# Where the matmuls' two operands start in a partition: weights at multiples of 512 bytes, the four input tiles at four other places

## Chip, core and metric

The kernel runs on one core of a Trainium2 chip. What counts is the device time in microseconds (us) of one execution. Matmuls run on TensorE (PE in the profile, its loads of the stationary operand PEld), the rest on VectorE (DVE), ScalarE (ACT) and GpSimd (POOL); SP only issues transfers. "Start" below always means the byte in a partition of the on-chip memory at which a tile begins, taken modulo 512.

## What is computed

Two decoder layers on 256 positions of width 2048, in float32. Each layer is a norm, one wide input projection, attention heads, a gate and an output projection that is added to the residual; a last norm follows. Cut to what matters here:

```
def layer_even(x, norm_g, w_in, w_out):
    h = rmsnorm(x, norm_g)
    qa, ka, va, iq, ik, iw, qb, kb, vb, gate = split_cols(h @ w_in, SPLIT0)
    ...   # two kinds of attention: o_a, o_b
    y = concatenate([o_a, o_b])
    return x + (y * silu(gate)) @ w_out
# layer_odd: the same with two other kinds of attention; then rmsnorm(x, norm_f)
```

## The kernel before

The work is a list of 39 jobs: 14 slices of the first input projection (heads B0 to B5, keys K, index I0 and I1, pairs A0 to A8), four of its output projection (P0 to P3), 17 of the second input projection (C0, F1, G1, C2 to C7, D0 to D7), and four of its output (Q0 to Q3). A job multiplies 256 rows by up to 512 columns over 16 blocks of depth 128 (`kt`). For each `kt` and each half `th` of the rows, `product` (L297 to L299) issues three matmuls that add into one PSUM tile. Every one has its own load of a 128x128 stationary operand, and this text calls the three a triple:

```
    nc.tensor.matmul(o, a, wh, ...)   # L297: stationary xh (or yh), moving whi
    nc.tensor.matmul(o, a, wl, ...)   # L298: stationary xh (or yh), moving wlo
    nc.tensor.matmul(o, b, wh, ...)   # L299: stationary xl (or yl), moving whi
```

Each operand is thus kept as a high and a low part in fp32r. `xh`, `xl` are the normed input of a layer's input projections, `yh`, `yl` the gated heads' output for the output projections. `whi`, `wlo` are the parts of the weights: a piece of weights lands in `raw` (1 MB, issued by SP in `load`), ACT copies it to `whi` (L263) and DVE subtracts to get `wlo` (L264), four buffers of each, up to three halves of a piece ahead of the matmuls. The first job's weights land in `w0yh`, `w0yl`, which lie in the place of `yh`, `yl`. In the last job, Q3, the weights of the first eight `kt` are put into the dead `xh`, `xl`, which are then the moving operand.

Heads run beside the projections as generators: `advance` lets them issue a few small matmuls between triples, in an order written out by `yield` counts. All instructions are in a hand-set order; where tiles lie changes no instruction.

Tiles are laid one behind the other: pool `cp` first, then `wp` (`raw`, `whi`, `wlo`), then `hp` (heads). Each size is rounded up to 32 bytes. The first tile of `cp` starts at 128. Adding up the declared sizes gives the starts before:

| tiles | start mod 512 |
|---|---|
| `cons`, `rt`, `xs` | 128 |
| `xh`, `xl`, `yh`, `yl` (16,384 bytes each, slices of 512 bytes) | 224 |
| `score` (1,536 bytes), `cT` (1,024) | 160, 288 |
| `raw`, `whi`, `wlo` (slices of 2,048 bytes at 512 columns) | 288 |
| `ikh`, `ikl`, `vA`, `tris`, `qkh`, `qkl` of the heads | 288 |
| `ih`, `il`, `sph`, `spl` of the heads | 480 |

A slice of 336 columns (job K) is 1,344 bytes, so that the second `kt` of a buffer starts at 288 + 1,344 = 96 mod 512; one of 264 columns (F1) at 320. `cT` holds a transposed sum of F1's forget gates; DVE writes it once (L657), and POOL sends it to DRAM (L658). `score` holds the index scores and then the mask of the A heads.

Of the kernel before, what the change touches and what calls it, by code (L numbers as in the profile page):

```python
# [7 lines left out]
F32 = mybir.dt.float32  # L8
BF16 = mybir.dt.bfloat16
F32R = mybir.dt.float32r  # L10
# [4 lines left out]
P = 128  # L15
NT = 2
SEQ = 256
D = 2048
KT = D // P
HD = 128  # L20
HA, HB, HC, HDD = 10, 6, 8, 8
# [132 lines left out]
    return np.ascontiguousarray(t.reshape(NT, P, -1).transpose(1, 0, 2).reshape(P, -1))  # L154


@with_exitstack
def trunk(ctx, tc, x, xT, g1, w0, wo0, w1, wo1, bf, gf, consts, rope, out):
    nc = tc.nc
    cp = ctx.enter_context(tc.tile_pool(name="cp", bufs=1))  # L160
# [4 lines left out]
    pa = ctx.enter_context(tc.tile_pool(name="pa", bufs=2, space=PSUM))  # L165
    ctx.enter_context(tc.manual_schedule())

    cons = cp.tile([P, CW], F32, name="cons")
    rt = cp.tile([P, NT, RW // 2], F32, name="rt")
    xs = cp.tile([P, NT, D], F32, name="xs")  # L170
# [10 lines left out]
    nmask = cons[:, 640:1024]  # L181
    bmask = cons[:, 1024:1408]
    smask = cons[:, 1408:1792]
    xh = cp.tile([P, KT, SEQ], F32R, name="xh")
    xl = cp.tile([P, KT, SEQ], F32R, name="xl")
    home = [cp.tile([P, KT * SEQ], F32, name=f"w0{n}", tag=n) for n in ("yh", "yl")]
    ys = []
    ss = cp.tile([P, 3, NT, 5], F32, name="ss")
    rstd = cp.tile([P, 3, NT], F32, name="rstd")
    mhalf = cp.tile([P, NT], F32, name="mhalf")  # L190
# [12 lines left out]
    score = cp.tile([P, 384], F32, name="score")  # L203
    nbA = score
    logf = cp.tile([P, NT, HDD], F32, name="logf")
    cq = cp.tile([P, NT, HDD], F32, name="cq")
    cT = cp.tile([HDD, SEQ], F32, name="cT")
    cTd = dr.tile([HDD, SEQ], F32, name="cTd")
    r0, r1, r2 = rstd[:, 0, :], rstd[:, 1, :], rstd[:, 2, :]
    BLK = ((0, slice(0, P)), (1, slice(P, 384)))  # L210
# [638 lines left out]
```

## Time and profile before

| | |
|---|---|
| time, median of 3 runs | 941.61 us (941.05 to 941.75) |
| time of the profiled execution | 941.87 us |
| its span | 940.1 us |
| PE busy, PEld busy | 925.9 us, 774.2 us |
| DVE, ACT, POOL busy | 591.5, 479.7, 43.9 us |
| matmuls | 4538 |

A matmul's length in the profile is that of one pass from its start to its modelled end, and consecutive ones overlap. What one costs in a stream is the distance between two starts, which the timeline shows to 0.01 us.

### The profile page before, as it was taken

What the parts mean: (1) busy time and instruction counts of PE and PEld (TensorE: products, weight loads), DVE (VectorE), ACT (ScalarE), POOL (GpSimd) and SP (SyncE); (2) the same over time, 40 slices, a digit from 0 to 9 for tenths busy, and PEclk for the clock granted to TensorE, in tenths of its full rate; (3) what the DMA queues carried; (4) which work ended last, traced back from release to release, by engine and by line L of the source; (5) the groups of instructions that cost most, each with busy time, mean ns of one, the idle gap of its engine ahead of it and who ended that gap; (6) DMA issues with size and microseconds to landing.
All of it is one profiled execution on the core that took longest, in us unless ns stands there. A gap on an engine that the chain in (4) does not pass through costs nothing.

```text
span 940.1 us, 11922 instructions
## 1 busy us (share of the span) xinstructions
PE 925.9 (98%) x4538; PEld 774.2 (82%) x4538; DVE 591.5 (63%) x978; ACT 479.7 (51%) x804; POOL 43.9 (5%) x63
## 2 busy tenths in 40 slices
PE   8899999999999999999999999999999999999996
PEld 5888888888888888888898888888888888888886
DVE  7467777766565665555567666666666666665552
ACT  7554454445445545545455555555555544554441
POOL 0002100000000000000000000000000000001110
PEclk9999999999999999999999999999999999999999
DMA  9765344443444445555456444445655555455542
GB/s 345 287 224 180 135 174 169 167 170 136 171 180 179 140 174 180 179 179 180 128 168 245 161 160 158 166 174 179 230 185 185 170 174 172 176 176 179 182 176 90
DMA packets 27177, 168.76 MB, mean 180 GB/s; under 512 B 3160, under 2 KB 3696, under 8 KB 8944
## 3 DMA queue, kind: packets, MB, share of 16 engines
q1 hardware_dynamic: 25920, 165.10, 49.7%
q0 software_dynamic: 768, 2.12, 0.8%
q8 instruction: 35, 0.57, 0.2%
q10 hardware_dynamic: 432, 0.79, 0.2%
q14 instruction: 22, 0.18, 0.1%
HBM read 165.89 MB, written 2.11 MB: 179 GB/s over the span
## 4 chain that ended last, share of the span: by engine, by line
PE 93%; DMA 3%; issue 2%; ACT 1%; DVE 1%; POOL 0%; SPq 0%; POOLq 0%; ACTq 0%; DVEq 0%
PE pj L297 28%; PE pj L299 28%; PE pj L298 28%; PE tp L355 3%; DMA raw<-in_w_in_dram 1%; DMA w0yl<-in_w_in_dram 1%; PE o L382 1%; PE o L383 1%; PE o L381 1%; ACT sq L421 1%; PE s L398 1%; DMA xst<-in_xT_dram 1%; PE s L372 0%; PE s L370 0%; PE s L371 0%
## 5 line engine op out<-in xcount | busy, mean ns | idle before, releaser
L264 DVE TENSOR_TENSOR wlo<-raw,whi 128x1024 fp32r<-128x1024 f32 (+3 forms) x300 | 356.2, 1197 | 223.6 <-ACT whi L263 223.3
L263 ACT ACTIVATE whi<-raw 128x1024 fp32r<-128x1024 f32 (+3 forms) x300 | 304.7, 1025 | 172.6 <-PE pj L299 155.6
L297 PE MATMUL pj<-whi,xh 128*128 128x512 f32 (+3 forms) x992 | 390.9, 394 | 0.9 <-ACT whi L263 0.9
L299 PE MATMUL pj<-whi,xl 128*128 128x512 f32 (+3 forms) x992 | 381.2, 384 | 0.0
L298 PE MATMUL pj<-wlo,xh 128*128 128x512 f32 (+3 forms) x992 | 379.5, 383 | 1.0 <-DVE wlo L264 1.0
L299 PEld LDWEIGHTS pj<-whi,xl 128*128 128x128 f32 x992 | 187.1, 189 | 37.9
L298 PEld LDWEIGHTS pj<-wlo,xh 128*128 128x128 f32 x992 | 187.7, 189 | 33.0 <-DVE wlo L264 1.8
L297 PEld LDWEIGHTS pj<-whi,xh 128*128 128x128 f32 x992 | 187.6, 189 | 32.3 <-ACT whi L263 2.3
L297 PE MATMUL pj<-whi,yh 128*128 128x512 f32 (+1 forms) x248 | 97.1, 392 | 0.0
L299 PE MATMUL pj<-whi,yl 128*128 128x512 f32 (+1 forms) x248 | 95.5, 385 | 0.0
L298 PE MATMUL pj<-wlo,yh 128*128 128x512 f32 (+1 forms) x248 | 94.8, 382 | 0.0
L299 PEld LDWEIGHTS pj<-whi,yl 128*128 128x128 f32 x248 | 46.6, 188 | 10.1
L298 PEld LDWEIGHTS pj<-wlo,yh 128*128 128x128 f32 x248 | 46.7, 188 | 9.0
L297 PEld LDWEIGHTS pj<-whi,yh 128*128 128x128 f32 x248 | 46.7, 188 | 8.2
L407 ACT ACTIVATE pr<-sn,nm 128x128 f32<-128x128 f32 (+1 forms) x48 | 21.5, 448 | 46.2 <-DVE nm L405 46.2
L391 ACT ACTIVATE yh<-tp 128x256 fp32r<-128x256 f32 x32 | 12.3, 384 | 47.1 <-PE tp L355 47.1
L632 DVE RECIPROCAL e<-e 128x256 f32<-128x256 f32 x16 | 28.0, 1753 | 0.5
L350 POOL TENSOR_TENSOR qk<-rot,rot 128x256 f32<-128x256 f32 x22 | 16.0, 741 | 239.2 <-DVE rot L349 239.2
L392 DVE TENSOR_TENSOR yl<-tp,yh 128x256 fp32r<-128x256 f32 x32 | 13.5, 423 | 19.9 <-ACT yh L391 19.9
L421 ACT ACTIVATE sq<-xs 128x512 f32<-128x512 f32 x23 | 14.3, 622 | 22.8 <-DVE xs L589 22.7
L364 ACT ACTIVATE qkh<-tp 128x384 fp32r<-128x384 f32 x22 | 10.8, 491 | 20.5 <-PE tp L355 20.5
L618 ACT ACTIVATE qk<-pj,rr 128x128 f32<-128x128 f32 x32 | 11.8, 368 | 15.9 <-PE pj L299 15.9
(201 smaller groups left out, 704.7 us busy)
## 6 DMA issues: line engine op xcount, KB each, us to landing
raw<-in_w_in_dram SPq DMA_DIRECT2D x108, 1024.0 KB, 4.8
raw<-in_w_out_dram SPq DMA_DIRECT2D x32, 1024.0 KB, 4.8
raw<-in_w_in_dram SPq DMA_DIRECT2D x4, 672.0 KB, 11.9
raw<-in_w_in_dram SPq DMA_DIRECT2D x4, 528.0 KB, 3.5
w0yl<-in_w_in_dram SPq DMA_DIRECT2D x4, 512.0 KB, 7.2
xs<-in_x_dram SPq DMA_DIRECT2D x2, 1024.0 KB, 11.9
raw<-in_w_in_dram SPq DMA_DIRECT2D x4, 512.0 KB, 3.9
xst<-in_xT_dram SPq DMA_DIRECT2D x6, 256.0 KB, 6.6
```

The costliest lines, as they stand in the source:

```text
L263: nc.scalar.activation(hi, rw, AF.Copy)
L264: nc.vector.tensor_tensor(lo, rw, hi.bitcast(F32), op=OP.subtract)
L297: nc.tensor.matmul(o, a, wh, start=(kt == 0), stop=False)
L298: nc.tensor.matmul(o, a, wl, start=False, stop=False)
L299: nc.tensor.matmul(o, b, wh, start=False, stop=(kt == KT - 1))
L350: nc.gpsimd.tensor_tensor(dst, t1[:, 0:n], t2[:, 0:n], op=OP.add)
L355: nc.tensor.transpose(pt[:, i * P:(i + 1) * P], s, ident)
L391: nc.scalar.activation(yh[:, kt, :], pt[:, 0:SEQ], AF.Copy)
L392: nc.vector.tensor_tensor(yl[:, kt, :], pt[:, 0:SEQ], yh[:, kt, :].bitcast(F32), op=OP.subtract)
L407: nc.scalar.activation(pr[:, s], sn[:, s], AF.Exp, scale=-1.0, bias=nm[:, th:th + 1], accum_out=l[:, th:th + 1])
L421: nc.scalar.activation(j, xs[:, th, c * 512:(c + 1) * 512], AF.Square, accum_out=ss[:, i, th, c:c + 1])
L632: nc.vector.reciprocal(e, e)
```

## The change

Four things, all of them about places:

- `xh`, `xl` and the homes of `yh`, `yl` are allocated first in `cp`, with fillers between, so that they start at 128, 256, 384 and 192.
- `cT` is no tile of its own any more but the first eight partitions and 256 columns of `score`.
- A filler of 672 bytes at the end of `cp` lets `wp` and `hp` start at a multiple of 512. Adding up sizes: `yl` ends at 192, the tiles from `cons` to `cq` bring the end to 352, and 672 bytes more make a multiple of 512. So `raw`, `whi`, `wlo` and the first tiles of `hp` start at 0; everything in `wp` and `hp` has moved by 224 bytes. `cons`, `rt`, `xs` start at 192.
- No instruction is added, removed or moved.

```diff
+PHASES = {"xh": 128, "xl": 256, "yh": 384, "yl": 192}
...
+    at, first = 128, {}
+    for n, ph in PHASES.items():
+        if ph != at:
+            cp.tile([P, (ph - at) % 512 // 4], F32, name=f"fill_{n}")
+        first[n] = cp.tile([P, KT * SEQ], F32R if n[0] == "x" else F32, name=n if n[0] == "x" else f"w0{n}", tag=n)
+        at = ph
+    xh, xl = (first[n].rearrange("p (a b) -> p a b", a=KT) for n in ("xh", "xl"))
+    home = [first[n] for n in ("yh", "yl")]
+    ys = []
...
-    xh = cp.tile([P, KT, SEQ], F32R, name="xh")
-    xl = cp.tile([P, KT, SEQ], F32R, name="xl")
-    home = [cp.tile([P, KT * SEQ], F32, name=f"w0{n}", tag=n) for n in ("yh", "yl")]
-    ys = []
...
-    cT = cp.tile([HDD, SEQ], F32, name="cT")
+    cT = score[0:HDD, 0:SEQ]
+    cp.tile([P, 168], F32, name="fill")
```

## Rows read from the trace of the kernel before

**Rows 1.** The page: span, and the share of each engine (busy us, share of the span, instructions).

```profile
span 940.1 us, 11922 instructions
PE 925.9 (98%) x4538; PEld 774.2 (82%) x4538; DVE 591.5 (63%) x978; ACT 479.7 (51%) x804; POOL 43.9 (5%) x63
PEclk9999999999999999999999999999999999999999
```

**Rows 2.** The chain that ended last, by engine; and three transfers of it at the start of the span (start us, length us, what).

```profile
PE 93%; DMA 3%; issue 2%; ACT 1%; DVE 1%; POOL 0%; SPq 0%; POOLq 0%; ACTq 0%; DVEq 0%
...
2.12 4.78 DMA xst<-in_xT_dram
7.28 7.26 DMA w0yl<-in_w_in_dram
17.25 13.83 DMA raw<-in_w_in_dram
```

**Rows 3.** Groups of PE's matmuls by shape: line, out<-moving,stationary, stationary shape, output, count | busy us, mean ns of one | idle before.

```profile
L297 PE MATMUL pj<-whi,xh 128*128 128x512 f32 x896 | 361.6, 404 | 0.9 <-ACT whi L263 0.9
L297 PE MATMUL pj<-whi,yh 128*128 128x512 f32 x232 | 92.7, 399 | 0.0
L297 PE MATMUL pj<-whi,xh 128*128 128x336 f32 x32 | 10.9, 342 | 0.0
```

**Rows 4.** Timeline of PE in the first pass of Q3 (start us, length us, line, what): the first and the last of 19 consecutive matmuls, stationary `yh`, `yl`.

```profile
915.52 0.40 PE L297 MATMUL pj<-whi,yh 128*128 128x512 f32 x1
...
919.64 0.39 PE L297 MATMUL pj<-whi,yh 128*128 128x512 f32 x1
```

**Rows 5.** Timeline of PE in job I1, with a triple of the index heads between two of the projection.

```profile
85.27 0.40 PE L297 MATMUL pj<-whi,xh 128*128 128x512 f32 x1
...
85.95 0.39 PE L528 MATMUL s<-ikh,ih 128*128 128x512 f32 x1
...
86.64 0.39 PE L297 MATMUL pj<-whi,xh 128*128 128x512 f32 x1
...
87.33 0.40 PE L297 MATMUL pj<-whi,xh 128*128 128x512 f32 x1
```

**Rows 6.** Timeline of PE in a C job: two 256-column matmuls of the stick head, and triples behind them.

```profile
586.15 0.28 PE L693 MATMUL s<-sph,tris 128*128 128x256 f32 x1
...
586.39 0.40 PE L297 MATMUL pj<-whi,xh 128*128 128x512 f32 x1
...
587.09 0.40 PE L297 MATMUL pj<-whi,xh 128*128 128x512 f32 x1
...
589.89 0.40 PE L297 MATMUL pj<-whi,xh 128*128 128x512 f32 x1
```

**Rows 7.** Timeline of PE in Q3, 256 columns: seven triples with moving `whi`, then eight with moving `xh`, `xl`, then seven with `whi` again (the starts of first and last).

```profile
923.20 0.28 PE L297 MATMUL pj<-whi,yh 128*128 128x256 f32 x1
...
925.67 0.28 PE L297 MATMUL pj<-whi,yh 128*128 128x256 f32 x1
...
926.03 0.28 PE L297 MATMUL pj<-xh,yh 128*128 128x256 f32 x1
...
928.89 0.28 PE L297 MATMUL pj<-whi,yh 128*128 128x256 f32 x1
...
931.37 0.28 PE L297 MATMUL pj<-whi,yh 128*128 128x256 f32 x1
```

**Rows 8.** Timeline of PE in Q3, 512 columns, moving `xh`: one triple at 908.80 and two at 911.58.

```profile
908.80 0.40 PE L297 MATMUL pj<-xh,yh 128*128 128x512 f32 x1
...
909.50 0.40 PE L297 MATMUL pj<-xh,yh 128*128 128x512 f32 x1
...
911.58 0.39 PE L297 MATMUL pj<-xh,yh 128*128 128x512 f32 x1
...
912.93 0.39 PE L297 MATMUL pj<-xh,yh 128*128 128x512 f32 x1
```

**Rows 9.** Timeline of PE in job K, 336 columns. The buffer's first `kt` starts at 288, its second at 96; each has two triples. Four triples from 29.64, and eight from 35.19.

```profile
29.64 0.32 PE L297 MATMUL pj<-whi,xh 128*128 128x336 f32 x1
...
30.56 0.31 PE L297 MATMUL pj<-whi,xh 128*128 128x336 f32 x1
...
31.48 0.32 PE L297 MATMUL pj<-whi,xh 128*128 128x336 f32 x1
...
35.19 0.32 PE L297 MATMUL pj<-whi,xh 128*128 128x336 f32 x1
...
36.10 0.32 PE L297 MATMUL pj<-whi,xh 128*128 128x336 f32 x1
...
37.04 0.32 PE L297 MATMUL pj<-whi,xh 128*128 128x336 f32 x1
...
37.96 0.32 PE L297 MATMUL pj<-whi,xh 128*128 128x336 f32 x1
...
38.89 0.32 PE L297 MATMUL pj<-whi,xh 128*128 128x336 f32 x1
```

**Rows 10.** Groups of ACT and DVE by shape (as rows 3): the splits of weights with source and target at different starts.

```profile
L263 ACT ACTIVATE whi<-raw 128x1024 fp32r<-128x1024 f32 x276 | 289.2, 1056 | 156.5 <-PE pj L299 146.2 <-ACT whi L263 6.6 <-ACT pT L412 2.0
L263 ACT ACTIVATE xh<-raw 128x1024 fp32r<-128x1024 f32 x4 | 4.0, 1046 | 0.0
L264 DVE TENSOR_TENSOR wlo<-raw,whi 128x1024 fp32r<-128x1024 f32 x276 | 338.8, 1236 | 204.4 <-ACT whi L263 204.2
L264 DVE TENSOR_TENSOR wlo<-w0yl,whi 128x1024 fp32r<-128x1024 f32 x4 | 4.9, 1225 | 0.0
```

**Rows 11.** One stretch (from:to us, length, busy us and instructions of PE, PEld, DVE, ACT, POOL, granted clock, share of the DMA engines, GB/s): in it a piece lands in `raw`.

```profile
587.10:589.80 2.70, 2.70 (x13) 2.22 (x12) 1.08 (x2) 1.56 (x2) 0.00 (x0) 1.00 1.01 416
```

**Rows 12.** All instructions on `score` and on `cT` (duration min/median/max ns, first and last start us): the last reader of `score`, the writer and the reader of `cT`.

```profile
L405 DVE CUSTOM_DVE_ANT_0 sn<-s,score x20: 282/355/421, 210.2 to 318.3; 128x128 f32<-128x128 f32 x10, 128x256 f32<-128x256 f32 x10
...
L657 DVE COPY cT<-s x1: 402/402/402, 493.6 to 493.6; 8x256 f32<-8x256 f32 x1
L658 POOL DMA_DIRECT2D cTd<-cT x1: 558/558/558, 494.3 to 494.3; - x1
```

## The prediction

> **What bounds the kernel now.** I read the page's engine shares first, then the chain that ended last, then the groups of matmuls by shape, then the timeline of PE at single places. The shares say that PE has work in flight for 925.9 of 940.1 us and that its granted clock is at 90% or more of 2.4 GHz in all 40 slices [rows 1]. The chain says the same from behind: 93% of it is PE, 3% transfers [rows 2]. So only two things can move the time by more than a little: the distance between two matmul starts, and the first 30 us, in which transfers are on the path. No other engine's speed matters, since ACT is busy for 51% and DVE for 63% of the span [rows 1].
>
> The groups give the counts: 896 triples of 512 columns with `xh`, `xl` and 232 with `yh`, `yl`, so 1,128; the 32 of 336 columns and the other narrow ones are a few per cent of the work [rows 3]. The group's 404 ns is no price, since passes overlap. The price is in the timeline: six triples in a row take 919.64 - 915.52 = 4.12 us, so a triple takes 686.7 ns and a matmul 228.9 [rows 4]. 512 columns at 2.4 GHz are 213.3 ns, so 15.6 ns of every matmul are something else. All that this change can give or take on PE is in that remainder: 1 ns a matmul is 1,128 x 3 = 3.4 us, 0.36% of the time.
>
> **What the change does to PE.** While one matmul streams its moving operand, PE loads the next one's stationary operand. What the change alters is how far apart the two start. I write d for the start of the stationary minus the start of the moving tile, modulo 512. Before, d is 224 - 288 = 448 for all four inputs. After, the weights start at 0, so d is 128 for `xh`, 256 for `xl`, 384 for `yh`, 192 for `yl`. The trace of before has other values of d in other matmuls, and these are the nearest rows:
>
> - d = 192 (index heads: 480 - 288). Their triple takes 86.64 - 85.95 = 0.69 us, between projection triples at d = 448 of 0.68 and 0.69 [rows 5]. No difference; this is `yl`'s new value.
> - d = 320 (stick heads, 288 - 480, 256 columns): two matmuls take 586.39 - 586.15 = 0.24 us [rows 6]. At d = 448, seven triples of 256 columns take 2.47 us, 117.6 ns a matmul [rows 7], two of them 0.235. No difference.
> - d = 0 (Q3, where `xh`, `xl` move and `yh`, `yl` are stationary, 256 columns): eight triples take 2.86 us, 357.5 ns each, between neighbours of 352.9 and 354.3 [rows 7]. That is 1.1% more, with the same stationary tiles. So starts are not without effect. At 512 columns the same pair gives 0.70 us for one triple and 0.675 for each of two others [rows 8].
> - d = 128 (job K, a buffer's second `kt`, which starts at 96): pairs of triples take 0.94 and 0.93 us against 0.91 and 0.92 for d = 448 in between, 2.2% more; but from 29.64 the two d take 0.92 and 0.92 [rows 9]. Until 31.08 ACT and DVE still wait for the transfer that starts at 17.25 [rows 2], so the difference later may be theirs. This is `xh`'s new value.
>
> d = 256 and 384 are in no row. Three values are equal to each other within what the rows resolve (448, 192, 320), one is worse by 1% on the whole but better in two triples (0), one is unclear (128). The remainder of 15.6 ns itself is there at d = 448, 192 and 320 alike, so it is not a matter of d. I take 0 for the 1,128 wide triples; the bounds are the fastest and the slowest triple seen, 675 and 700 ns, or -12 and +13 ns a triple.
>
> The slow triple occurs at d = 448 too: behind the stick head's matmuls four triples take 589.89 - 587.09 = 2.80 us, 700 ns each [rows 6]. What sets it off there is what came before, since the starts are the same as ever.
>
> The Trainium skill (TensorE: Matmul & The Clock Gate, step-by-step of what each phase is for) says that PE has two independent read ports, one for the moving operand and one for the load, and that loading the next operand takes no bandwidth from the running matmul. By that alone the change is worth 0 and the 1.1% of `xh` in Q3 could not be; the trace shows it, so the measurement decides, and I keep the bounds.
>
> **The other parts.** Splits: ACT takes 1056 ns with source and target at 288 and 1046 with the target at 224; DVE takes 1236 and 1225 with other sources [rows 10]. At most 1%, on engines that PE's work covers; without that cover, 10 ns for each of 276 + 276 would be 5.5 us, but ACT and DVE idle before these splits for 156 and 204 us. 0.
>
> Transfers: pieces land in `raw` at 0 instead of 288. Three transfers of 4.78 + 7.26 + 13.83 = 25.9 us are on the path at the start [rows 2]. With `raw` at 288 a stretch shows the DMA engines fully busy at 416 GB/s [rows 11], so a start that is no multiple of 512 does not hold them far below their best. I take -0.2 us, with 0 and -0.8 (3% of 25.9) as bounds.
>
> `cT` in `score`: the last reader of `score` is DVE at 318.3 us; DVE itself writes `cT` at 493.6, and POOL's transfer reads it at 494.3 [rows 12]. No later instruction writes `score`. DVE does both in its order, so no wait is added on any queue. 0.
>
> Narrow and mixed places: in K the second `kt` now starts at 320 and d becomes 128 - 320 = 320, one of the quiet values which returns 20 ns in some of its 8 pairs of triples, 0.1 us; in Q3 d becomes 256, 128 or 64 instead of 0, 16 triples at 4.6 ns, 0.1 us. Taken as -0.1 together, bounds -0.2 and +0.2.
>
> **The sum.** 941.87 (the profiled execution: 940.1 of span and 1.8 around it) + 0 - 0.2 - 0 - 0.1 = 941.6; the median of the runs lies 0.26 lower than that execution, so 941.3 against 941.61. I forecast no change that can be told: about 0.2% (1.9 us) is what a measurement of this kernel can tell. This case's own range is 939.7 to 943.5.
>
> **Rivals.**
>
> *Faster, because collisions go.* If the load and the stream hinder each other where they come near, then d = 448 is only 64 bytes from d = 0, and all new values are further away. For it: d = 0 does cost 1.1% [rows 7], and the 700 ns triples would be a collision that a small shift in time brings about. Removing only what is seen to collide (some 60 triples of 13 ns, the edges around the heads) gives 1 to 2 us; if the wide triples also go from 686.7 to the 675 of two triples [rows 8], 1,128 x 11.7 ns = 13.2 us, 928. I put it halfway at 934. Against it: 448, 192 and 320 give the same triple, so distance does nothing beyond 64 bytes.
>
> *Faster, because a start at a multiple of 512 is read faster.* 256 more columns cost 228.9 - 117.6 = 111.3 ns [rows 4, 7], 0.435 a column, where 2.4 GHz gives 0.417. If the 4.3% above it came from starts inside a 512-byte row, 0.018 x 512 = 9.3 ns would go from each of 3,384 matmuls: 31 us, 910. Against it: moving starts of 288 and 480 have the same price [rows 5, 6], and a price by column is not what a first row cut short would give. The Trainium skill (TensorE: Matmul & The Clock Gate, back-to-back issue gap) gives N / 2.4 + 2.5 ns, 215.8 for 512 columns; by it the stream has 13 ns too much, and an estimate with it for all 3,384 would be 44 us less. No run here shows a 512-column stream at that distance.
>
> *Slower, because the new distances collide.* The place is `xh`: d = 128 is the value that looked slow in K [rows 9], and it holds for L297 and L299's streams. If two of three matmuls in 896 triples go to the price of the 700 ns triple, that is 2/3 x 13.3 x 896 = 7.9 us, 949.3; with all four inputs colliding 1,128 x 13.3 = 15 us, 956. It decides as soon as the mean triple is over 688.4 ns (1.9 us / 1,128 = 1.7). Against it: the first part of K shows nothing of it, and three of the four values with clean rows are quiet.
>
> **Chances.** No change that can be told 0.40; collisions go 0.26; fast rows 0.08; new collisions 0.26. So faster 0.34, same 0.40, slower 0.26. The predicted time is 941.3. The range takes in half a price beyond the collision rivals on both sides but neither extreme (910; 956): 927 to 951, which leaves out about 0.08 below and 0.07 above, with a little on each side for prices that no row shows.
>
> **What would show it.** Right: the triple in Q3's first pass at 686 to 688 ns, the groups of PE with the same means, the first matmul of job K at the same time within 0.5 us. The rivals show in the same place: 675 or 700 ns a triple in projections with `xh`, and then a difference between `xh` jobs (d = 128, 256) and `yh` jobs (384, 192) tells which d it is; a distance near 219 ns in all of them would be the rows. The forecast is wrong if the triples lock differently over long stretches: what sets off the 700 ns behind the stick heads is not understood, and it could appear or vanish behind any head with the new starts.

## The result and the profile after

The changed kernel takes 951.66 us (median; 951.44 to 952.32), the kernel before beside it 941.68 (941.05 to 942.27). The ratio is 1.0107, its 95% interval 1.0091 to 1.0123: slower by 1.07%, 9.98 us. The forecast was no change, 941.3, with a range to 951.

In the page of the changed kernel I read the span and the engines' shares, as in [rows 1].

```profile
span 949.6 us, 11922 instructions
...
PE 938.0 (99%) x4538; PEld 773.7 (81%) x4538; DVE 591.8 (62%) x978; ACT 480.0 (51%) x804; POOL 43.9 (5%) x63
PEclk9999999999999999999999999999999999999999
```

PE has the same 4,538 matmuls and works on them for 12.1 us longer; the other engines are unchanged within half a microsecond. The same stretch of 350 us in both kernels, first the kernel before, then the changed one (from:to us, length, busy us and instructions of PE, PEld, DVE, ACT, POOL, granted clock, share of the DMA engines, GB/s), shows it most simply:

```profile
50.00:400.00 350.00, 350.00 (x1702) 291.55 (x1701) 227.23 (x439) 174.54 (x294) 25.14 (x34) 1.00 0.48 169
```

```profile
50.00:400.00 350.00, 350.00 (x1684) 287.94 (x1683) 225.22 (x435) 173.58 (x293) 25.11 (x34) 1.00 0.48 167
```

PE is never idle in either, the granted clock is 1.00 in both, which is the level of 2.4 GHz, and 18 matmuls fewer get done: 1.07%, the same share as in the result. No wait and no clock accounts for that here; each matmul takes longer. The timelines of PE in the changed kernel say by how much. A C job with `xh`, `xl`, nine triples' first matmuls (the first and the last shown; line 306 is line 297 of before):

```profile
584.77 0.39 PE L306 MATMUL pj<-whi,xh 128*128 128x512 f32 x1
...
590.37 0.39 PE L306 MATMUL pj<-whi,xh 128*128 128x512 f32 x1
```

Eight triples in 5.60 us, 700 ns each. The place in Q3 that answers to [rows 4], with `yh`, `yl`:

```profile
925.27 0.40 PE L306 MATMUL pj<-whi,yh 128*128 128x512 f32 x1
...
929.48 0.39 PE L306 MATMUL pj<-whi,yh 128*128 128x512 f32 x1
```

Six triples in 4.21 us, 702 ns, where before had 4.12 and 687. The groups of matmuls by shape hardly show it (columns as in [rows 3]):

```profile
L306 PE MATMUL pj<-whi,xh 128*128 128x512 f32 x896 | 363.0, 405 | 0.5 <-ACT whi L272 0.5
L306 PE MATMUL pj<-whi,yh 128*128 128x512 f32 x232 | 93.4, 403 | 0.0
```

405 against 404 and 403 against 399 ns: the length of one record holds its overlap with the next, and only the distance of starts is a price.

Other engines and transfers are not what makes the triples longer. In three triples of Q3 the rows show no work of DVE, ACT, POOL or DMA at all; first the kernel before, then the changed one, then e5 below, where all four inputs and the weights start at 0 (columns as above):

```profile
918.27:920.32 2.05, 2.05 (x10) 1.69 (x9) 0.00 (x0) 0.00 (x0) 0.00 (x0) 1.00 0.00 0
```

```profile
928.08:930.17 2.09, 2.09 (x10) 1.69 (x9) 0.00 (x0) 0.00 (x0) 0.00 (x0) 1.00 0.00 0
```

```profile
913.34:915.37 2.03, 2.03 (x10) 1.68 (x9) 0.00 (x0) 0.00 (x0) 0.00 (x0) 1.00 0.00 0
```

The triples take 687, 700 (703, 704 and 693) and 680 ns there, as elsewhere.

I took the distance from each matmul's start to the next start over all triples of the two traces. "Clean" triples are wide ones from 50 us on with no head's matmuls directly ahead or behind. Where the 9.54 us of span (949.64 - 940.10) are:

| part | before us | after us | change |
|---|---|---|---|
| first job, 32 triples | 24.12 | 25.49 | +1.36 |
| 551 clean wide triples with `xh`, `xl` | 378.98 | 385.57 | +6.60 (12.0 ns each) |
| 200 clean wide triples with `yh`, `yl` | 137.33 | 139.95 | +2.62 (13.1 ns each) |
| 353 other wide triples: next to heads' matmuls, or with moving `xh` in Q3 | | | +1.75 |
| job K, 32 triples | 18.91 | 15.73 | -3.17 |
| narrow triples, heads' matmuls, tail | | | +0.39 |

So 11.0 us are lost in wide triples from 50 us to the end, 1.4 in the first job, and 3.2 come back in K's triples. Of the 1.4 only 0.3 are of the same kind (27 triples by 12 ns); 1.0 lies in the first five triples, two of which start 1.28 us apart in the changed kernel's timeline of PE, where before had 0.69:

```profile
7.12 0.63 PE L306 MATMUL pj<-whi,xh 128*128 128x512 f32 x1
...
8.40 0.63 PE L306 MATMUL pj<-whi,xh 128*128 128x512 f32 x1
...
9.68 0.59 PE L306 MATMUL pj<-whi,xh 128*128 128x512 f32 x1
10.10 0.40 PE L307 MATMUL pj<-wlo,xh 128*128 128x512 f32 x1
10.34 0.39 PE L308 MATMUL pj<-whi,xl 128*128 128x512 f32 x1
```

That is 0.43 us a matmul, what 512 columns take at 1.2 GHz; from 10.10 on it is 0.24. The trace's first record of the granted clock, at 1.00, starts at 10.09 us, and no record covers the time before it. In the kernel before the first record starts at 4.66. All 14 traces agree: in seven (the changed kernel, e3, e4, e5, e7, e9, e11) the first record starts at 9.3 to 10.4 us and the job's second triple takes 1.28 us; in the other seven it starts at 4.0 to 5.3, and that triple takes 0.69 to 0.71. e2 below has the distances of the change and is of the second kind. So this 1.0 us goes with the clock and not with d; what decides when the clock rises was not tried.

In K the stretch of 20 us, first of the kernel before, then of the changed one:

```profile
30.00:50.00 20.00, 17.43 (x105) 16.92 (x103) 12.14 (x21) 13.77 (x31) 2.11 (x3) 0.91 0.67 248
```

```profile
30.00:50.00 20.00, 18.68 (x115) 17.48 (x114) 12.68 (x24) 13.79 (x32) 2.12 (x3) 1.00 0.68 252
```

Before, PE waited longer for POOL in this stretch, until 44.15 us, and its granted clock then fell to 0.50, the level of 1.2 GHz, from 45.62 to 49.03:

```profile
45.62:49.03 3.41, 3.41 (x14) 3.41 (x13) 3.32 (x5) 3.13 (x5) 0.00 (x0) 0.50 0.56 151
```

The waits of PE on POOL (who waits <- releaser: us, count, longest), of before and of after:

```profile
PE tp L355 <- POOL qk L350: 2.6, 2, 2.3
```

```profile
PE tp L364 <- POOL qk L359: 0.7, 2, 0.5
```

In the changed kernel PE comes 1.3 us later to the wait (its last triple ahead of it starts at 42.52 instead of 41.21) and POOL starts 0.5 us earlier (42.83 instead of 43.37), so the wait is 1.9 us shorter. The clock stays at 1.00, where three of K's triples had taken 840 ns and one 785 before, against 460 to 470 elsewhere. What was lost ahead of the wait was got back there, with the price of the clock on top. Behind K's last triple 0.9 us of it are lost again, 0.6 in a wait for DVE's `qkl`: from K's first matmul to the next job's first it is 20.36 us before and 18.07 after, so K as a whole returns 2.3 us.

### The profile page after: what moved, and what is told of

Read it like the earlier page. It is cut to its first block, busy times and chain, and to the rows that moved or that the text cites. A ratio compares the mean times of both kernels' runs of the same rounds, so it can differ in the third digit from the quotient of the medians.

```text
span 949.6 us, 11922 instructions
## 1 busy us (share of the span) xinstructions
PE 938.0 (99%) x4538; PEld 773.7 (81%) x4538; DVE 591.8 (62%) x978; ACT 480.0 (51%) x804; POOL 43.9 (5%) x63
## 4 chain that ended last, share of the span: by engine, by line
PE 91%; DMA 3%; DVE 2%; issue 2%; ACT 2%; SPq 0%; POOL 0%; POOLq 0%; ACTq 0%; DVEq 0%
PE pj L307 27%; PE pj L308 27%; PE pj L306 27%; PE tp L364 3%; DMA raw<-in_w_in_dram 1%; DMA w0yl<-in_w_in_dram 1%; PE o L391 1%; PE o L392 1%; PE o L390 1%; ACT sq L430 1%; DVE wlo L273 1%; PE s L407 1%; DMA xst<-in_xT_dram 1%; PE s L380 0%; PE s L381 0%
```

## The experiments

All of them leave the computation as it is; they move buffers. Theories: *distance* (the triple's price depends on the start of the stationary minus that of the moving tile) and *place* (it depends on where a buffer starts by itself). Each of e3 to e12 is the changed kernel with the edit shown, and the weights stay at 0, except where a `gap` moves `wlo`. The means named below are over clean triples (some 550 with `xh`, `xl` and 200 with `yh`, `yl` in each run), from the distances of starts.

**e1, e2: everything shifted.** In e1 the kernel before gets one tile in front, so that all starts move by 224 bytes: weights 0, inputs 448, d still 448. In e2 the changed kernel gets one of 288 bytes: weights 288, inputs 416, 32, 160, 480, d as in the change.

```diff
 e1: before
+    cp.tile([P, 56], F32, name="front")
 e2: after
+    cp.tile([P, 72], F32, name="front")
     at, first = 128, {}
```

> The kernel before with 224 unused bytes in front of everything: weights start at 0, the four inputs at 448, all distances between tiles as before. Theory 'distance' (only d, the start of the stationary minus that of the moving tile modulo 512, counts; d stays 448): 941.7 us within 0.2%, wide triples of 686 to 687 ns. Theory 'absolute start' (a moving tile that starts at a multiple of 512, or of 64, costs more): 951 to 952 us, triples of 700 ns.

> The changed kernel with 288 unused bytes in front of everything: weights start at 288 as before, inputs at 416, 32, 160, 480, so d is 128, 256, 384, 192 as in the change. Theory 'distance': 951.7 us, triples of 700 ns. Theory 'absolute start': 941 to 942 us, 687 ns.

e1: 940.72 us against 941.40, ratio 0.9994 (0.9983 to 1.0005). e2: 952.31, ratio 1.0112 (1.0083 to 1.0142). Timeline of PE, first e1 (six triples in 4.12 us, 687 ns), then e2 (eight in 5.60, 700 ns):

```profile
415.36 0.39 PE L298 MATMUL pj<-whi,yh 128*128 128x512 f32 x1
...
419.48 0.39 PE L298 MATMUL pj<-whi,yh 128*128 128x512 f32 x1
```

```profile
585.25 0.39 PE L307 MATMUL pj<-whi,xh 128*128 128x512 f32 x1
...
590.85 0.39 PE L307 MATMUL pj<-whi,xh 128*128 128x512 f32 x1
```

All weights at multiples of 512 alone do nothing, and moving them off again repairs nothing. Distance is right; place falls, for the two shifts tried. e1 also shows the granted clock at 1.00 from 30 to 50 us, with the distances of before, and of the 14 traces e3 and e8, with other distances, have a fall in K like before's (from 44.12 and from 44.96 us); so that fall is not a matter of d.

**e3, e4: four more distances.**

```diff
 e3
+PHASES = {"xh": 192, "xl": 192, "yh": 320, "yl": 320}
 e4
+PHASES = {"xh": 64, "xl": 64, "yh": 0, "yl": 0}
```

> The changed kernel with xh and xl at 192, yh and yl at 320, weights at 0. The rows of before showed d = 192 (index heads) and d = 320 (stick heads) as quiet. Theory 'distance': triples of about 687 ns in both kinds of job, 941 to 943 us. Theory 'absolute start': 700 ns in both, 951 to 952 us.

> The changed kernel with xh and xl at 64, yh and yl at 0, weights at 0. Theory 'distance': d = 0 gives over 690 ns in the y jobs (Q3 of before showed 1.1% more at d = 0); d = 64 is in no row; if only the size of the distance counts it is as 448, 687 ns, so 942 to 945 us. Theory 'absolute start': 700 ns in both kinds, 951 to 952 us.

e3: 943.51 against 941.40; triples 687.8 (d = 192) and 699.9 (320). e4: 947.84; 700.0 (64) and 681.1 (0). Both times lie above the ranges given for 'distance', because three of the four prices expected were wrong, for 320, 64 and 0; but 'absolute start' asked 700 ns in both kinds of job of both runs, and two of the four are far below it. Timeline of PE in e3 (320: six triples, 4.20 us) and in e4 (0: six triples, 4.08 us):

```profile
415.53 0.40 PE L306 MATMUL pj<-whi,yh 128*128 128x512 f32 x1
...
419.73 0.40 PE L306 MATMUL pj<-whi,yh 128*128 128x512 f32 x1
```

```profile
415.50 0.39 PE L306 MATMUL pj<-whi,yh 128*128 128x512 f32 x1
...
419.58 0.39 PE L306 MATMUL pj<-whi,yh 128*128 128x512 f32 x1
```

d = 320, which I had called quiet, is slow at 512 columns. d = 0, which Q3 had shown worse by 1.1%, is the best seen. Both of my rows were of 256 columns [rows 6, 7]; the row of 512 columns at d = 0 [rows 8] had its two triples of 0.675 us (679.5 ns by unrounded starts), and I gave them no weight. At 256 columns the order is another: in the narrow part of Q3 a triple takes 360 ns at d = 0 (e5), 354 at 448 (before), 359 at 384 (the changed kernel), 346 at 320 (e3).

**e5 to e8: the best one everywhere, and the course.** e5 puts all four inputs at 0; e6 asks whether 512 or 256 is the period; e7 and e8 look next to the good values.

```diff
 e5
+PHASES = {"xh": 0, "xl": 0, "yh": 0, "yl": 0}
 e6
+PHASES = {"xh": 256, "xl": 256, "yh": 128, "yl": 128}
 e7
+PHASES = {"xh": 480, "xl": 480, "yh": 32, "yl": 32}
 e8
+PHASES = {"xh": 96, "xl": 96, "yh": 160, "yl": 160}
```

> The changed kernel with all four inputs and the weights at 0, so d = 0 everywhere. In the run with yh, yl at d = 0 the wide y triples took 681 ns against 687 at d = 448. Theory 'distance': x jobs do the same, 680 to 682 ns; 896 + 232 triples at 6 ns less are 6.8 us, so 934 to 936 us, faster than the kernel before. Rival 'd = 0 is good only with yh, yl' (their jobs differ in what runs beside them): x jobs at 687 to 700 ns, 940 to 952 us.

> The changed kernel with xh, xl at 256 and yh, yl at 128. Theory 'period 256' (448 and 192 gave 687 and 688 ns, 64 and 320 both 700): d = 256 is as 0, so x triples 680 to 682 ns; d = 128 is as 384, 700 in the y jobs; 937 to 939 us. Rival 'period 512': d = 256 is the farthest from 0 and another value altogether, anything from 687 to 700.

> The changed kernel with xh, xl at 480 and yh, yl at 32, the steps between d = 448 (687), 0 (681) and 64 (700). Theory 'distance in a smooth course': x 681 to 687 ns, y 681 to 700. Rival 'steps of 64 bytes, and anything between two steps straddles both': each at the worse of its neighbours, x 687, y 700. 936 to 941 us or 939 to 943.

> The changed kernel with xh, xl at 96 and yh, yl at 160, between 64 (700), 128 (700 if the changed kernel's xh is what costs) and 192 (688). Smooth course: x 700 ns, y 688 to 700, 950 to 952 us. Rival 'steps': x 700, y 700.

e5: 936.72 us (936.24 to 936.89) against 941.44, ratio 0.9947 (0.9931 to 0.9964): faster than both kernels. It has every part of the change, `cT` in `score` and the moved weights and heads included, but for the four starts; so the loss lies in these. e6: 939.57. e7: 951.86. e8: 954.55. Timeline of PE in e5, with `xh` (four triples in 2.72 us) and then in e6 (d = 256, three in 2.04), 680 ns both:

```profile
588.80 0.39 PE L306 MATMUL pj<-whi,xh 128*128 128x512 f32 x1
...
591.52 0.39 PE L306 MATMUL pj<-whi,xh 128*128 128x512 f32 x1
```

```profile
589.74 0.39 PE L306 MATMUL pj<-whi,xh 128*128 128x512 f32 x1
...
591.78 0.39 PE L306 MATMUL pj<-whi,xh 128*128 128x512 f32 x1
```

Timeline of PE in e7 (d = 480, nine triples in 6.30 us, 700 ns) and e8 (d = 96, seven in 4.93, 704 ns):

```profile
584.28 0.40 PE L306 MATMUL pj<-whi,xh 128*128 128x512 f32 x1
...
590.58 0.39 PE L306 MATMUL pj<-whi,xh 128*128 128x512 f32 x1
```

```profile
586.41 0.40 PE L306 MATMUL pj<-whi,xh 128*128 128x512 f32 x1
...
591.34 0.39 PE L306 MATMUL pj<-whi,xh 128*128 128x512 f32 x1
```

The means of clean 512-column triples, where high and low part of an input have the same d:

| d | 0 | 32 | 64 | 96 | 128 | 160 | 192 | 256 | 320 | 448 | 480 |
|---|---|---|---|---|---|---|---|---|---|---|---|
| ns | 681, 683 | 700 | 700 | 703 | 699 | 700 | 688 | 683 | 700 | 687, 688 | 700 |
| kernel | e4, e5 | e7 | e4 | e8 | e6 | e8 | e3 | e6 | e3 | before, e1 | e7 |

0 and 256 agree, 64 and 320 agree, 192 and 448 agree: every pair tried that is 256 apart has one price. Over these values there are two dips, at 0 (most triples 680) and at 192 (687), and 700 elsewhere. The course is not smooth: 480 lies between 448 and 0 and is worse than either. 'Steps' asked 687 there and falls as well, though it was right for 32 and 160. Each of the four runs misses the ranges written down for its time: e5 by 0.7 us and e6 by 0.6, their `xh` triples at 683 ns on the mean instead of 680 to 682; e7 by 9 and e8 by 2.6.

**e9 to e12: which of the pairs counts.** A triple has three matmuls, `whi` over `xh`, `wlo` over `xh`, `whi` over `xl`. Either each matmul's own stationary and moving tile matter (own pairs), or the tile that streams and the one that is loaded meanwhile for the next matmul (concurrent pairs: `whi` with `xh`, `wlo` with `xl`, `whi` with `xh`). e10 and e12 move `wlo` too, by a small tile ahead of the first.

```diff
 e9
+PHASES = {"xh": 128, "xl": 0, "yh": 0, "yl": 128}
 e10
+PHASES = {"xh": 0, "xl": 128, "yh": 0, "yl": 128}
+                if i == 0:
+                    wp.tile([P, 32], F32, name="gap", tag="gap", bufs=1)
 e11
+PHASES = {"xh": 128, "xl": 448, "yh": 448, "yl": 192}
 e12
+PHASES = {"xh": 0, "xl": 192, "yh": 0, "yl": 192}
+                if i == 0:
+                    wp.tile([P, 16], F32, name="gap", tag="gap", bufs=1)
```

> The changed kernel with xl, yh and the weights at 0, xh at 128, yl at 128. In the x jobs the high part alone is moved off d = 0, in the y jobs the low part alone. Theory 'the load that runs under a stream collides with it': xh is loaded under two of three streams (L306's and L308's moving whi), yl under one (L307's moving wlo). x triples near 700 as in the changed kernel, y triples between, 685 to 695. Rival 'one bad pair sets the beat of all three': 700 ns in both. Rival 'only the high part matters': y triples 681. Time 948 to 952 us, as x is four fifths of the work.

> The changed kernel with xh, yh, whi at 0 and xl, yl, wlo all at 128. Streams and the loads that run under them are then at d = 0 (whi with the loads of xh, wlo with that of xl), but a matmul's own pair is not (L307: wlo with xh, L308: whi with xl). Theory 'the load that runs under a stream': 680 to 683 ns in both kinds, 936 to 938 us. Rival 'a matmul's own two operands': about 700 ns, 949 to 953 us.

> The changed kernel with xl and yh at 448 and yl at 192 (both values gave 687 ns), weights at 0, and xh at 128 as in the change. Theory 'distance, each pair for itself': y triples 687 as before, x triples near 700 from xh alone; 949 us. Rival 'it takes both parts off': x triples 690 to 695, 945 us.

> The opposite of the run with all low parts at 128: xh, yh, whi at 0, xl and yl at 192, wlo at 64. A matmul's own pairs are all at good distances (L306: 0; L307, wlo with xh: 192; L308, whi with xl: 192), but the stream of wlo has the load of xl under it at 192 - 64 = 128. Theory 'a matmul's own two operands': triples of 680 to 687 ns, 937 to 942 us. Theory 'the load that runs under a stream': one of three streams collides, 690 to 695 ns, 944 to 948 us. In the run before both came out halfway (693), so a third result, again near 693 here, would mean that both pairs count.

e9: 951.04 against 942.22. With `xh` at 128 and `xl` at 0 a triple takes 700.3 ns; with `yh` at 0 and `yl` at 128 it takes 693.8. That is as 'the load that runs under a stream' asked; neither 'one bad pair sets the beat' (700 in both) nor 'only the high part' (681 with `yh`) holds. e11: 948.35; `xh` alone at a bad distance gives 698.6, while the `y` triples, 448 with 192, stay at 686.8. In these two runs the high part alone costs nearly the whole price, the low part alone about two thirds (693.8 between 681 and 700). Timeline of PE in e11, first `yh` (six triples in 4.12 us), then `xh` (seven in 4.91, 701 ns):

```profile
415.31 0.39 PE L306 MATMUL pj<-whi,yh 128*128 128x512 f32 x1
...
419.43 0.39 PE L306 MATMUL pj<-whi,yh 128*128 128x512 f32 x1
...
583.60 0.40 PE L306 MATMUL pj<-whi,xh 128*128 128x512 f32 x1
...
588.51 0.40 PE L306 MATMUL pj<-whi,xh 128*128 128x512 f32 x1
```

e10: 946.12. All concurrent pairs have d = 0, two of three own pairs 128 or 384; the triples take 693.1 and 693.2, steadily 693 in some stretches and by turns 682 and 705 in others. e12: 948.71 against 941.41. All own pairs have d = 0, 448 or 192, one concurrent pair 128 (`wlo` with `xh` is at 448, where the expectation says 192); the triples take 695.5 and 698.8, slower than either theory asked. Timeline of PE in e10 (five triples in 3.46 us, 692 ns) and e12 (four in 2.80, 700 ns):

```profile
415.67 0.40 PE L308 MATMUL pj<-whi,yh 128*128 128x512 f32 x1
...
419.13 0.40 PE L308 MATMUL pj<-whi,yh 128*128 128x512 f32 x1
```

```profile
416.20 0.40 PE L308 MATMUL pj<-whi,yh 128*128 128x512 f32 x1
...
419.00 0.40 PE L308 MATMUL pj<-whi,yh 128*128 128x512 f32 x1
```

Good concurrent pairs alone don't make a good triple, nor do good own pairs alone. The steps inside a triple agree. In e9's `yh` triples the three distances of starts are 227.6, 232.2 and 234.0 ns, against 227.4, 226.7 and 226.7 in e5: the middle step, with the load at 128 under it, and the last, with its own pair at 128 but the load under it at 0, both grow. In e12's `yh` triples they are 233.1, 231.0 and 234.8, so even the first is longer, with both of its pairs at 0. Neither theory holds in its pure form, and which combination counts stays open. So does what in the memory makes the levels 680, 687 and 700; no run looks inside it.

## Why the prediction was wrong

**The step that failed** is the 0 for the 1,128 wide triples, where 11.0 us were lost in those from 50 us on, 12.0 ns a clean triple with `xh` and 13.1 with `yh`. It was made of three readings, and two of them were of the wrong shape.

1. *d = 192 and 320 are quiet.* 192 is (687.8 in e3), and its row was of 512 columns. 320 is not (699.9); its row was two matmuls of 256 columns [rows 6]. At 256 columns a distance has another price than at 512, and I carried it over.
2. *d = 128 is unclear.* Job K showed it 2% worse in two of the four pairs from 35.19 us, and I put that down to ACT and DVE [rows 9]. It was d. In K's steady part the slow pairs of triples are those of each buffer's second `kt` before (d = 128: 0.934 us, against 0.919 at 448) and those of its first `kt` in the changed kernel (d = 128: 0.938, against 0.929 at 320). At 512 columns it is 698.6 to 700.3 against 687 to 688 ns, 1.6 to 1.8%.
3. *The 15.6 ns are there at three values of d alike, so they are not a matter of d.* This is the wrong conclusion proper. 12.0 to 13.1 ns a triple were lost by d alone, and 4 to 6 gained at d = 0 in e4 and e5. "Three of four values are quiet" was a sample of two, and by the table only 4 of the 11 distances are as good as before's 448 or better, that one included.

**The rivals.** *New distances collide* was right in mechanism and close in size: its price of 13.3 ns for all four inputs is 12.0 and 13.1 as measured, and its places, the `xh` jobs, showed 700 ns as it asked. It gave 949.3 for `xh` alone and 956 for all; 951.66 lies between them, but for another reason: the triples of both pairs are slow (through `xh` and `yh`: in e11, with quiet low parts, `xh` still at 128 leaves 698.6 ns, and `yh` at 448 instead of 384 gives 686.8), and K gave 2.3 us back. That the time fell so near the range, which ended 0.66 us short, is in part luck: without K's share it would have been farther out. *Collisions go* had the sign of "near" wrong: 0 and 256 are the best values, not the worst, and 64 bytes away from 0 there is 687 on the one side (448), 700 on the other (64). e5 comes nearest to its 934, with 936.72, 4.7 us under the kernel before, but by making all distances 0. *A start at a multiple of 512* falls by e1, where the weights have such starts: ratio 0.9994. The 44 us that the prediction sets beside it rest on a formula that the Trainium skill (TensorE: Matmul & The Clock Gate, back-to-back issue gap) gives for an isolated matmul, not for a stream with a load for each; the shortest distance of a steady stream here is 226.7 ns (680 / 3, at d = 0 in e5).

The rule of two independent read ports in the Trainium skill (TensorE: Matmul & The Clock Gate, step-by-step of what each phase is for), by which the load takes nothing from the running matmul, does not explain these runs: 680 and 700 ns come from the same instructions with buffers shifted. I had kept a bound against it, but took its result as the likely one.

**The terms that held.** The price bounds of -12 and +13 ns a triple hold, within half a nanosecond, for the mean of all but e8's 703. The transfers at the start, of the changed kernel in the chain that ended last:

```profile
2.12 4.85 DMA xst<-in_xT_dram
7.37 7.41 DMA w0yl<-in_w_in_dram
...
17.41 13.21 DMA raw<-in_w_in_dram
```

25.5 us against 25.9: -0.4, within the 0 to -0.8 given. `cT` in `score` brought no new wait on the chain; ACT and DVE are busy as before. The narrow part of Q3 went as small as forecast, +0.04 in all. K was not in the sum with more than 0.1 us: I had read its triples for d and not asked what a later PE does to its wait for POOL. That term is worth -2.3 us in these two executions. Of the 1.9 us by which the wait shrank, 1.3 are PE's later arrival and 0.5 POOL's earlier start. The other traces bear this out: PE starts its last triple ahead of the wait at 41.2 to 42.5 us in all 14, and the first triple behind it starts at 44.2 to 45.1 in all, no later where PE came late. How much K returns differs between executions: e2, with the distances of the change and its clock at 1.00 there too, takes 18.99 us for it.

**What would show it** did show it: 702 instead of 686 to 688 ns in Q3's first pass. The mean of the group was a bad test, as said above. K's first matmul came 1.2 us later (30.86 against 29.64), not within 0.5, mostly by the first job's five slow triples, the 1.0 us that goes with the clock, which no step of mine foresaw.

## What to carry to other kernels

Where PE is the bound and streams 512-column fp32r tiles back to back, with a load of its own for every matmul, set the starts of stationary and moving buffers so that their difference is a multiple of 256 bytes, and read the triple from start to start; here that is worth 0.5% over the kernel before and 1.6% over a bad choice. Don't take a price for an operand's position from a matmul of another width. And ask of any loss ahead of a wait whether the wait gives part of it back.

## What was not expected of the hardware

- The distance between the starts of the two operands sets the time of a 512-column matmul in a steady stream: 226.7 ns at d = 0 and 256 (680 / 3), 229 at 192 and 448, 233.3 at most others. Where both start in absolute terms changed nothing (e1, e2).
- Wherever two values 256 apart were tried (0, 64, 192 with their partners), they agree within 3 ns a triple.
- At 256 columns the order is another: 360 ns a triple at d = 0 (the best at 512 columns), 354 at 448, and 341 to 349 at 64 and 320 (e3, e7, e8; slow at 512 columns).
- Behind a head's matmuls the triples take their time to settle: behind the stick head in a C job of e5 they take 703, 691, 691 and then 680 ns. In before, at the same place [rows 6], they take 703 and then 700 up to the next head's matmuls, so at d = 448 a stream can stay at 700 as well. What sets that off is still not shown.
